# The gate/up product of a SwiGLU feed-forward by one level of Strassen's scheme, with six groups of feed-forward chunks instead of three

## The chip, the cores and the metric

The kernel runs on one core of a Trainium2 chip. The metric is the device time in microseconds of one execution of the whole two-layer trunk. Three runs of the kernel before took 1856.1, 1854.63 and 1850.46 us; the median is 1854.63 us.

The engines are named as the profile names them: PE multiplies matrices, DVE and POOL (GpSimd) and ACT (ScalarE) work elementwise on up to 128 partitions, SP issues the DMAs, and PSUM is the memory into which PE accumulates.

## The reference

One step of a small trunk with 640 tokens (128 context tokens and 512 latent tokens) of width 1024, in fp32. Layer 0 mixes the tokens by differential attention, layer 1 by a gated recurrence; each mixer is followed by a feed-forward of width 2816:

```python
def adanorm(x, g, shift, scale):
    return rmsnorm(x, g) * (1.0 + scale) + shift

def swiglu(h, w_in, w_out):
    gt, up = jnp.split(h @ w_in, 2, axis=-1)
    return (jax.nn.silu(gt) * up) @ w_out
...
        mp = modulation(c_ctx, w_ada[i], b_ada[i])      # six vectors: shift, scale, gate, twice
        ms = modulation(c, w_ada[i], b_ada[i])
...
        xp = xp + mp[2] * op                            # op, os_: the mixer's output
        xs = xs + ms[2] * os_
        xp = xp + mp[5] * swiglu(adanorm(xp, g_norm_ffn[i], mp[3], mp[4]), w_ffn_in[i], w_ffn_out[i])
        xs = xs + ms[5] * swiglu(adanorm(xs, g_norm_ffn[i], ms[3], ms[4]), w_ffn_in[i], w_ffn_out[i])
```

The change concerns `h @ w_in`: a 640x1024 by 1024x5632 product per layer.

## The kernel before

**Numbers.** Every fp32 operand of a large product is split into a high part and a low part in the type fp32r, and a product is three matmuls: high by high, low by high, high by low. For a weight chunk, ACT copies the raw fp32 chunk into the high part (`wh`), and DVE or POOL subtracts that from the raw chunk to get the low part (`wl`); the function is `load_split`. On POOL the subtraction is cut into three instructions. Raw chunks lie in a ring `wr` of 3 buffers of 512 KB, high and low parts in rings `wh` and `wl` of 6 buffers each.

**Feed-forward.** It is `out_and_ffn`, once per layer. The features of h lie on the partitions: `hT` is a pair (`Thi`, `Tlo`) of 8 blocks of 128 features by 640 tokens. The width 2816 is cut into 22 chunks of 128, each called f. For one f, `ffn_chunks` loads two raw chunks of 512 KB (four feature blocks each, the gate and the up columns side by side) and splits both. `ffn_in` then works on one half of the tokens (320) at a time: 24 matmuls into one PSUM sum for the gate, 24 into another for up, both called `psgu`; ACT takes the silu of the gate, DVE multiplies the up sum by it, ACT and DVE split the product into the high and low parts of `gT`. The 22 f's are in three groups:

```python
FF_GROUPS = [(0, 8), (8, 15), (15, 22)]
```

After each group, `rows_out` multiplies `gT` by the rows of `w_ffn_out` of that group: for each half of the 1024 output columns and each of 5 token tiles one PSUM sum `psr` of 128x512, which DVE multiplies by the gate vector (`rtmp`, L1291) and adds to the rows of the residual (L1292).

**Ahead of the first group** the rows of the mixer's output are finished and normalised tile by tile, and each tile is turned by PE (`ntp`), scaled and shifted by DVE and POOL (`ha`, L492 and L493) and split by ACT and DVE (L494, L495) into `hT`; that is `to_hT`. The raw chunks of the first f are asked for when the second token tile is done.

**Work that runs beside the feed-forward.** `fill` is a chain of 64 small steps. The first eight take the last modulation vector of the layer itself: each loads one 512 KB chunk of `w_ada` and multiplies it on PE into the sum `psada`. In layer 0, the others are `summed_units`, modulation vectors of layer 1 computed on DVE: a chunk of `w_ada` is multiplied by the condition and added to an accumulator, which takes two TENSOR_SCALAR (L291) or SCALAR_TENSOR_TENSOR (L293, `acc`) instructions of 128x512 for each feature block, 20 and 140 in all. `take(fill)` issues the next step. It stands after each half of an f and after each tile of `rows_out`, so that the steps are spread over the three groups of layer 0.

**What sets the order.** The kernel is written as one program; a planner then orders the instructions of each engine by its own estimate of durations and due times, and adds the waits. In the places where `pe["strict"]` is set, PE keeps the written order: from the mixer's output until the first f's of the first group. Each engine takes its instructions in the order given; an instruction that waits holds up all that stand behind it on that engine.

## Time and profile before

| what | before |
|---|---|
| median of three runs | 1854.63 us |
| the profiled execution, its span | 1850.6 us (the profile gives no other time of its own for it) |
| PE busy | 1807.3 us, 98% of the span |
| DVE busy | 1081.6 us, 58% |
| ACT busy | 678.6 us, 37% |
| POOL busy | 439.3 us, 24% |
| first gate/up product of layer 0 / of layer 1 | from 437.23 us / from 1390.32 us |
| matmuls of the gate/up product | 4224, all of 128x320 |

Busy time of an engine is the time in which at least one of its instructions ran. Matmuls overlap in the records: one is shown with 309 ns, though another starts every 147 ns; for what a matmul takes of the span, the time of a whole run of them is divided by their number. The granted clock of PE is full from the second of the profile's 40 slices to the last. In layer 0 the feed-forward's groups run from 437 us to 912 us, in layer 1 from 1390 us to the end.

### The profile page before, as it was taken

What the parts mean: (1) busy time and instruction counts of PE and PEld (TensorE: products, weight loads), DVE (VectorE), ACT (ScalarE), POOL (GpSimd) and SP (SyncE); (2) the same over time, 40 slices, a digit from 0 to 9 for tenths busy, and PEclk for the clock granted to TensorE, in tenths of its full rate; (3) what the DMA queues carried; (4) which work ended last, traced back from release to release, by engine and by line L of the source; (5) the groups of instructions that cost most, each with busy time, mean ns of one, the idle gap of its engine ahead of it and who ended that gap; (6) DMA issues with size and microseconds to landing.
All of it is one profiled execution on the core that took longest, in us unless ns stands there. A gap on an engine that the chain in (4) does not pass through costs nothing.

```text
span 1850.6 us, 34604 instructions
## 1 busy us (share of the span) xinstructions
PE 1807.3 (98%) x14064; PEld 1664.6 (90%) x14064; DVE 1081.6 (58%) x1947; ACT 678.6 (37%) x1510; POOL 439.3 (24%) x620
## 2 busy tenths in 40 slices
PE   6999999999999999999999999999999999999998
PEld 5799999778998998999899999998789989998996
DVE  4888888756258546755666666676562333234234
ACT  3567666635231222122533333333352311212221
POOL 3345444325000000000255555555240000000001
PEclk8999999999999999999999999999999999999999
DMA  9511211554364434534422222212242422213211
GB/s 315 174 44 52 72 50 49 167 170 123 96 188 144 130 103 129 168 114 126 140 81 64 64 65 64 64 55 85 84 123 83 149 80 81 69 58 96 87 46 57
DMA packets 218363, 190.02 MB, mean 103 GB/s; under 512 B 9891, under 2 KB 176213, under 8 KB 218204
## 3 DMA queue, kind: packets, MB, share of 16 engines
q1 hardware_dynamic: 217398, 187.22, 32.7%
q8 instruction: 110, 1.80, 0.4%
q10 hardware_dynamic: 806, 0.60, 0.1%
q14 instruction: 49, 0.40, 0.1%
HBM read 180.40 MB, written 7.37 MB: 101 GB/s over the span
## 4 chain that ended last, share of the span: by engine, by line
PE 85%; DVE 7%; DMA 4%; ACT 2%; issue 1%; POOL 1%; SPq 0%; POOLq 0%; ACTq 0%; DVEq 0%
PE psgu L74 31%; PE psr L74 18%; PE psqkv L74 8%; PE psf L74 8%; PE psvg L74 5%; PE pso L74 3%; PE S L74 2%; PE pa L74 2%; PE po L74 1%; DMA wr<-w_ffn_in 1%; PE psada L74 1%; PE ptp L77 1%; DVE Q L1147 1%; DMA wr<-w_ada 1%; DMA ar<-w_ada 1%
## 5 line engine op out<-in xcount | busy, mean ns | idle before, releaser
L74 PE MATMUL psgu<-Tlo,wh 128*128 128x320 f32 x1408 | 435.0, 309 | 1.8 <-DVE Tlo L495 1.8
L74 PE MATMUL psgu<-Thi,wh 128*128 128x320 f32 x1408 | 436.5, 310 | 0.0
L74 PE MATMUL psgu<-Thi,wl 128*128 128x320 f32 x1408 | 434.7, 309 | 0.0
L167 ACT ACTIVATE wh<-wr 128x1024 fp32r<-128x1024 f32 (+1 forms) x224 | 225.9, 1015 | 416.0 <-DMA wr<-w_ffn_in 143.7
L171 DVE TENSOR_TENSOR wl<-wr,wh 128x1024 fp32r<-128x1024 f32 (+2 forms) x146 | 173.5, 1191 | 229.1 <-ACT wh L167 226.3
L74 PEld LDWEIGHTS psgu<-Thi,wh 128*128 128x128 f32 x1408 | 264.2, 188 | 5.7 <-issue 5.3
L74 PEld LDWEIGHTS psgu<-Tlo,wh 128*128 128x128 f32 x1408 | 264.2, 188 | 2.9 <-DVE Tlo L495 2.3
L74 PEld LDWEIGHTS psgu<-Thi,wl 128*128 128x128 f32 x1408 | 264.2, 188 | 0.0
L171 POOL TENSOR_TENSOR wl<-wr,wh 128x341 fp32r<-128x341 f32 (+2 forms) x234 | 218.6, 964 | 183.7 <-ACT wh L167 183.1
L74 PE MATMUL psr<-wh,Thi 128*128 128x512 f32 (+1 forms) x607 | 240.8, 398 | 0.5 <-ACT Thi L503 0.5
L74 PE MATMUL psr<-wh,Tlo 128*128 128x512 f32 (+1 forms) x607 | 235.8, 390 | 0.0
L74 PE MATMUL psr<-wl,Thi 128*128 128x512 f32 (+1 forms) x607 | 234.8, 388 | 0.0
L460 POOL TENSOR_TENSOR nss<-nss 128x1 f32<-128x1 f32 x24 | 7.5, 313 | 855.8 <-ACT xr L455 839.8
L74 PEld LDWEIGHTS psr<-wh,Tlo 128*128 128x128 f32 x607 | 114.3, 188 | 25.1
L74 PEld LDWEIGHTS psr<-wh,Thi 128*128 128x128 f32 x607 | 114.5, 189 | 24.8 <-issue 2.2
L74 PEld LDWEIGHTS psr<-wl,Thi 128*128 128x128 f32 x607 | 114.4, 188 | 21.8
L74 PE MATMUL psf<-Thi,wh 128*128 128x320 f32 x384 | 123.0, 320 | 0.0
L1394 DVE TENSOR_TENSOR gu<-psgu,sil 128x320 f32<-128x320 f32 x88 | 42.8, 486 | 134.0 <-PE psgu L74 134.0
L74 PE MATMUL psf<-Tlo,wh 128*128 128x320 f32 x384 | 118.5, 309 | 0.0
L74 PE MATMUL psf<-Thi,wl 128*128 128x320 f32 x384 | 118.5, 308 | 0.0
L74 PE MATMUL psqkv<-wh,Thi 128*128 128x384 f32 x320 | 109.1, 357 | 1.2 <-ACT Thi L596 1.2
L1291 DVE TENSOR_TENSOR rtmp<-psr,gate 128x512 f32<-128x512 f32 x69 | 47.3, 688 | 102.6 <-PE psr L74 99.4
(250 smaller groups left out, 3440.0 us busy)
## 6 DMA issues: line engine op xcount, KB each, us to landing
wr<-w_ffn_in SPq DMA_DIRECT2D x176, 256.0 KB
wr<-w_ada SPq DMA_DIRECT2D x72, 512.0 KB
wr<-w_ffn_out SPq DMA_DIRECT2D x40, 512.0 KB
wr<-w_in_rec SPq DMA_DIRECT2D x64, 256.0 KB
wr<-w_qkv_attn SPq DMA_DIRECT2D x64, 192.0 KB
ar<-w_ada SPq DMA_DIRECT2D x24, 512.0 KB
gate<-gdram SPq DMA_DIRECT2D x12, 512.0 KB
wr<-w_o_attn SPq DMA_DIRECT2D x8, 512.0 KB
```

Source lines behind the costliest of these rows:

```text
L74: in_order(nc.tensor.matmul(*a, **k))
L77: in_order(nc.tensor.transpose(*a, **k))
L167: nc.scalar.activation(hi[:, :n], r, AF.Copy)
L171: ins = lo_eng.tensor_tensor(lo[:, cs], r[:, cs], hi[:, cs], ALU.subtract)
L460: nc.gpsimd.tensor_tensor(sq[1], sq[0], sq[1], ALU.add)
L1147: nc.vector.tensor_tensor(qview, qview, view(T, n + 1, [2, nb], [-n - 1, 2], [0, m]), ALU.mult)
L1291: nc.vector.tensor_tensor(tmp, ps, gates[0 if t == 0 else 1][:, cs], ALU.mult)
L1394: nc.vector.tensor_tensor(gu, pss[1], sil, ALU.mult)
```

## The change

For one f, the product of the token halves and the feature halves with gate and up is taken as a product of 2x2 blocks: rows are the tokens 0-319 and 320-639, the inner index is the feature halves (blocks 0-3 and 4-7), columns are gate and up. In place of the 8 block products of 4 feature blocks each (12 matmuls each, 96 in all) there are 7 (84 in all), on sums and differences of blocks.

- **The tokens' side, once per layer.** `A1` holds the high and low parts of the tokens 0-319, `A22` those of tokens 320-639 for the feature blocks 4-7, and `S` those of four sums and differences, which lie in the storage of the mixer's output `oT`. `to_rows` takes the place of `to_hT`; `sums` makes the four sums, one addition on POOL and three on DVE per stretch of tokens, in tiles of the tag "row" (3 buffers).
- **The weights' side, for each f.** `ffn_weights` loads the same two raw chunks. POOL makes four differences of 128x512 (L1397 to L1400) into two tiles of the tag "row". Four splits follow (of 512, 1024, 1024 and 1024 elements per partition, ACT L168 and DVE L169), where there were two of 1024.
- **The products.** `ffn_in` is now one routine for both halves of the tokens, with three places for a step of `fill`. Seven products go in the order 1, 2, 6, 5, 7, 3, 4. Three of the sums are carried on in PSUM: `psgu` takes 1, then 6, 7 and 4; `psu` takes 5, then 3; `psg` takes 2. After 1, 6, 5 and 7, ACT copies the sum so far to SBUF (`p1`, `u2`, `p5`, `u3`; L1447 to L1462), and the next product into the same sum follows that copy. DVE adds and multiplies (L1450, L1465, L1466, L1472), POOL adds one (L1463), ACT takes two silus (L1451, L1471), and `out` splits the two results (L1441, L1442) into `gT`.
- **Groups.** Six instead of three: `FF_GROUPS = [(0, 4), (4, 8), (8, 12), (12, 16), (16, 19), (19, 22)]`. `rows_out` thus runs 12 times per layer, not 6; it makes the same number of matmuls for `w_ffn_out`. The second instruction of a row's addition goes to POOL, except in the last half of a layer.
- **`fill`.** A place after each tile of `rows_out` as before, so there are twice as many of these, and three places per f instead of two.
- **The start.** The raw chunks of the first f are asked for after the first three steps of `fill`, not before them. Their low parts are made on DVE, not POOL.
- **Storage.** Gates are loaded in halves of 512 columns; `ha`, `gate`, `rtmp`, `xc` and `acc` share a tag "h" of 7 buffers; `gT` has one buffer, shared with the unsplit `Hf`; the two pools of mixer storage become one; three tables of attention are made in attention's own pool.

The core of the diff:

```diff
-FF_GROUPS = [(0, 8), (8, 15), (15, 22)]
+FF_GROUPS = [(0, 4), (4, 8), (8, 12), (12, 16), (16, 19), (19, 22)]
...
-            def add_rows(ps, t, half, gates):
+            def add_rows(ps, t, half, gates, eng=nc.vector):
...
-                nc.vector.tensor_tensor(xs[t][:, cs], xs[t][:, cs], tmp, ALU.add)
+                eng.tensor_tensor(xs[t][:, cs], xs[t][:, cs], tmp, ALU.add)
...
-                    add_rows(ps, t, half, gates)
+                    add_rows(ps, t, half, gates, nc.gpsimd if after is None else nc.vector)
                     take(fill)
...
+            def sums(c0, c1):
...
+                nc.gpsimd.tensor_tensor(fa[:, 0], a21, a22, ALU.add)
+                nc.vector.tensor_tensor(fa[:, 1], a11, a21, ALU.subtract)
+                nc.vector.tensor_tensor(fb[:, 0], fa[:, 0], a11, ALU.subtract)
+                nc.vector.tensor_tensor(fb[:, 1], a12, fb[:, 0], ALU.subtract)
+                for i, f in enumerate((fa, fb)):
+                    split_rows([v[:, 2 * i : 2 * i + 2, :, c0:c1] for v in S], f)
+
+            def ffn_weights(f):
+                cols = slice(f * P, (f + 1) * P)
+                r1, r2 = (load_raw(wi[:, 4 * c : 4 * c + 4, :, cols], [4, 2, P]) for c in range(2))
...
+                h1 = split(b11, nc.vector, [4, P])
+                h2 = split(x2, nc.vector, [4, 2, P])
+                ta, tb = (xr_tile().rearrange("p (s k c) -> p s k c", s=2, k=4) for _ in range(2))
+                nc.gpsimd.tensor_tensor(ta[:, 0], b12, b11, ALU.subtract)
+                nc.gpsimd.tensor_tensor(ta[:, 1], b22, b12, ALU.subtract)
+                nc.gpsimd.tensor_tensor(tb[:, 0], b22, ta[:, 0], ALU.subtract)
+                nc.gpsimd.tensor_tensor(tb[:, 1], b21, tb[:, 0], ALU.subtract)
+                tb, ta = (
+                    split(t.rearrange("p s k c -> p (s k) c"), nc.vector, [8, P]) for t in (tb, ta)
+                )
...
+            def ffn_in(f, w, group, i):
...
+                sum1 = mm_tile([P, HTOK], "psgu")
+                product(sum1, 1, True)
+                a = part_tile("p1")
+                nc.scalar.activation(a, sum1, AF.Copy)
+                ps = mm_tile([P, HTOK], "psg")
+                product(ps, 2, True)
+                nc.vector.tensor_tensor(a, a, ps, ALU.add)
+                nc.scalar.activation(a, a, AF.Silu)
+                yield
+                product(sum1, 6, False)
...
+                yield
+                product(sum1, 4, False)
...
             for t in range(NT):
...
-                if t == 1:
-                    first = [ffn_chunks(0, nc.gpsimd, l == 0)]
...
                 if gi == 0:
                     take(fill, 3)
-                    first.append(ffn_chunks(1, nc.vector))
-                    to_hT(NT - 2)
-                    ffn_in(0, first[0], gT, 0, 0)
-                    to_hT(NT - 1)
+                    weights = [ffn_weights(0)]
+                    to_rows(NT - 2, nc.vector)
+                    units = [ffn_in(0, weights[0], group, 0)]
+                    take(units[0])
+                    weights.append(ffn_weights(1))
+                    to_rows(NT - 1, nc.vector)
...
                 for f in range(max(f0, 2), f1):
-                    ch = ffn_chunks(f)
-                    for half in range(2):
-                        ffn_in(f, ch, gT, f - f0, half)
+                    for _ in ffn_in(f, ffn_weights(f), group, f - f0):
                         take(fill)
```

Two places show how the order of the instructions moves. The first is SP's order of DMAs at the end of the mixer's output in layer 0. A name such as `wr_5739` is one raw buffer in use; a `w_ffn_in` chunk has two rows because it is loaded by two DMAs of 256 KB. Before:

```order
L69 DMA wr_5571<-w_o_attn 128x2x512 [waits DMAHW2_49,PE_49]
L69 DMA wr_5739<-w_ffn_in 128x4x128 [waits DMAHW7_49,DMAHW3_49,PE_49]
L69 DMA wr_5739<-w_ffn_in 128x4x128
L69 DMA wr_5748<-w_ffn_in 128x4x128 [waits DMAHW5_49,DVE_49]
L69 DMA wr_5748<-w_ffn_in 128x4x128
L69 DMA wr_5943<-w_ada 128x1024 [waits DMAHW6_49,DVE_49]
```

After, with the three chunks of `w_ada` (steps of `fill`) first:

```order
L69 DMA wr_5571<-w_o_attn 128x2x512 [waits DMAHW2_49,PE_49]
L69 DMA wr_5927<-w_ada 128x1024 [waits DMAHW7_49,DMAHW3_49,PE_49]
L69 DMA wr_5933<-w_ada 128x1024 [waits DMAHW5_49,DVE_49]
L69 DMA wr_5939<-w_ada 128x1024 [waits DMAHW6_49,DVE_49]
...
L69 DMA wr_5945<-w_ffn_in 128x4x128 [waits PE_49]
L69 DMA wr_5945<-w_ffn_in 128x4x128
L69 DMA wr_5948<-w_ffn_in 128x4x128 [waits DMAHW5_49,PE_49]
```

The first f's chunks now stand behind the three `w_ada` chunks, and their first DMA waits for PE: for the products `psada` that read the buffer before it. On PE those products stand here in both kernels, after the last `psr` of the mixer's output. What PE has next in the changed kernel, with the single rows of a product left out after its first two:

```order
L74 MATMUL psada_5926<-wr_5939,cT_91 32x256 x4
L77 MATMUL ntp_5973<-ident_66,xr_5845 128x128 x4
...
L74 MATMUL psgu_5999<-A1hi_5609,wh_5951 128x320
L74 MATMUL psgu_5999<-A1lo_5610,wh_5951 128x320
...
L74 MATMUL psada_5926<-wr_6174,cT_91 32x256 x4
L74 MATMUL psgu_6084<-A1hi_5609,wh_6035 128x320
L74 MATMUL psgu_6084<-A1lo_5610,wh_6035 128x320
L74 MATMUL psada_5926<-wr_6197,cT_91 32x256 x4
```

Before, 48 gate/up products in a row follow the first `ntp` pair, and no `psada` stands among them; now further `psada` products, each with a raw chunk of its own, stand between the products of the first two f's.

The second place is DVE in layer 0, amid `fill`. Before, among the f's of the first group:

```order
L1394 TENSOR_TENSOR gu<-psgu,sil 128x320
L291 TENSOR_SCALAR acc<-wr,cT 128x512 x2
L293 SCALAR_TENSOR_TENSOR acc<-wr,cT,acc 128x512
L1396 TENSOR_TENSOR Tlo<-gu,Thi 128x320
L293 SCALAR_TENSOR_TENSOR acc<-wr,cT,acc 128x512 x8
L171 TENSOR_TENSOR wl<-wr,wh 128x1024
```

After, at the end of the first group's `rows_out`s and the start of the second group:

```order
L1317 TENSOR_TENSOR rtmp<-psr,gate 128x512
L169 TENSOR_TENSOR wl<-wr,wh 128x512
L303 SCALAR_TENSOR_TENSOR acc<-wr,cT,acc 128x512 x4
L169 TENSOR_TENSOR wl<-wr,wh 128x1024
L303 SCALAR_TENSOR_TENSOR acc<-wr,cT,acc 128x512 x2
L1450 TENSOR_TENSOR p_7818<-p_7818,psg 128x320
L303 SCALAR_TENSOR_TENSOR acc<-wr,cT,acc 128x512
L169 TENSOR_TENSOR wl<-xr,wh 128x1024
```

There are more splits (`wl`) between the same number of accumulations (`acc`). All 160 `acc` instructions, which before lie in all three groups of layer 0 (22 f's), stand in the changed kernel within the first three of six groups (12 f's).

More of the change, by code (lines that the diff above doesn't have):

```diff
@@ L160, in load_raw, with split @@
         return r[:, :n]
+    def split(src, lo_eng, dims):
+        n = int(np.prod(dims))
+        out = []
+        for name in ("wh", "wl"):
+            v = wp.tile([P, 1024], F32R, name=name, tag=name, bufs=6)[:, :n]
+            if len(dims) == 2:
+                v = v.rearrange("p (a b) -> p a b", a=dims[0])
+            else:
+                v = v.rearrange("p (a b c) -> p a b c", a=dims[0], b=dims[1])
+            out.append(v)
+        nc.scalar.activation(out[0], src, AF.Copy)
+        lo_eng.tensor_tensor(out[1], src, out[0], ALU.subtract)
+        return out
     def load_split(src, dims, lo_eng, ordered=False, slots=None):
@@ L1326, in last_head @@
+            gates = [half_gates(0, half) for half in range(2)]
             def last_head(t):
@@ L1376, in out_and_ffn @@
             nxt = None
[L1378 to L1396 removed]
+            group = {}
```

222 lines of the change are left out of this document (148 added, 74 removed).

## The prediction

> **What bounds the kernel now.** I read the page first (busy shares, the 40 slices, the chain's shares, the product's group), then the chain in order of time, then busy time by stretches of the span.
>
> ```profile
> span 1850.6 us, 34604 instructions
> PE 1807.3 (98%) x14064; PEld 1664.6 (90%) x14064; DVE 1081.6 (58%) x1947; ACT 678.6 (37%) x1510; POOL 439.3 (24%) x620
> DVE  4888888756258546755666666676562333234234
> POOL 3345444325000000000255555555240000000001
> PE 85%; DVE 7%; DMA 4%; ACT 2%; issue 1%; POOL 1%; SPq 0%; POOLq 0%; ACTq 0%; DVEq 0%
> L74 PE MATMUL psgu<-Tlo,wh 128*128 128x320 f32 x1408 | 435.0, 309 | 1.8 <-DVE Tlo L495 1.8
> ```
>
> PE is busy 98% and carries 85% of the chain; so PE bounds, and taking matmuls away shortens the span as long as no other engine fills what is freed. DVE is at 2 to 8 tenths through layer 0's feed-forward (slices 10 to 20) and at 2 to 4 in the last ten, layer 1's; POOL is idle in both places. The last row is one of three such groups of the gate/up product. Its 309 ns is not a matmul's price, since matmuls overlap. The chain has that:
>
> ```profile
> 437.23 7.17 PE psgu L74 x47
> 453.45 20.73 PE psgu L74 x140
> 748.45 3.97 DMA wr<-w_ffn_in
> 1493.56 54.95 PE psr L74 x240
> 1548.51 98.55 PE psgu L74 x672
> ```
>
> 672 products in 98.55 us are 0.1467 us each; an output matmul (`psr`, 128x512) takes 54.95/240 = 0.229 us. One raw chunk of 512 KB, waited for alone, takes about 4 us to come.
>
> ```profile
> core 0: us, PE busy (x) PEld busy (x) DVE busy (x) ACT busy (x) POOL busy (x), PEclk, DMA share, GB/s
> 437.00:912.00 475.00, 474.31 (x3019) 439.44 (x3020) 271.67 (x407) 125.05 (x200) 10.56 (x17) 1.00 0.43 131
> 100.00:330.00 230.00, 229.76 (x1531) 222.06 (x1530) 191.10 (x453) 154.10 (x438) 104.12 (x192) 1.00 0.18 54
> 1549.00:1647.00 98.00, 98.00 (x670) 98.00 (x669) 29.54 (x43) 26.39 (x42) 0.00 (x0) 1.00 0.27 81
> 1038.00:1086.00 48.00, 47.29 (x616) 45.08 (x615) 32.72 (x62) 16.87 (x47) 24.91 (x28) 1.00 0.22 62
> ```
>
> In layer 0's groups (first row) PE loses 0.7 of 475 us, with DVE at 57%; in a group of layer 1 (third) DVE is at 30%. In attention (second) DVE ran at 83% with POOL at 45% and PE still lost nothing. The fourth row is a stretch of layer 1's mixer that I need below.
>
> **The change, part by part.** I add to the median, 1854.63; the profiled span is 4.0 under it.
>
> *Matmuls.* 12 fewer for each of 44 f's: 528 x 0.1467 = **-77.4 us**, if PE stays the bound. At the group's 309 ns it would be 163, which is wrong for the reason above. The output products keep their number.
>
> *The start of each feed-forward.* The rows at which the first f's of layer 0 begin:
>
> ```profile
> 433.05 1.50 PE L74 MATMUL psada<-wr,cT 128*32 128x256 f32 x24
> 433.75 7.74 SPq L69 DMA_DIRECT2D wr<-w_ffn_in  x8
> 437.65 1.06 ACT L167 ACTIVATE wh<-wr 128x1024 fp32r<-128x1024 f32 x1 [0.37 <-DMA wr<-w_ffn_in]
> 440.07 1.06 ACT L167 ACTIVATE wh<-wr 128x1024 fp32r<-128x1024 f32 x1
> 435.27 1.35 POOL L493 TENSOR_TENSOR ha<-ha,adaC 128x512 f32<-128x512 f32 x1 [0.45 <-DVE ha L492]
> ```
>
> Before, these two splits are of the second f; the first f was split long ago. Now the first f's chunks wait until `psada` at 433.05 has read the ring, so they take those places: 437.65 and 440.07. On POOL, behind the second chunk, stand this f's three later differences, the next f's four and a sum, each about 1.35: the first f's end near 444, the last about 452. The next step of `fill` gets its ring slot only near 444 and lands 4 us later; its `psada` stands in PE's order among the second f's products, and three more follow through the ring about 4 us apart: 448, 452, 456, and a last near 460. What is queued on PE behind them are the products of f 0 and 1, and of these only 48 (7 us) stand ahead. By 456 the kernel before had done 47+52+17 = 116 of them, by the chain. So (116 - 48) x 0.147 = 10 us are lost, and about 3 more for the last chunk: **+13 per layer, +26** for both, since layer 1 has the same order. Bounds: +8 each if one chunk more is hidden, +18 if one more is bare. Of the SP queue, the gates and `xc` that now stand behind those three `w_ada` chunks are small and not late by the same row (433.75).
>
> *Layer 0's groups 0 to 2.* These hold all of `fill`'s accumulations. PE needs 12 x 84 x 0.1467 + 360 x 0.229 + some 6 for `psada` = 236 us; with the start, 249. DVE's load, from forms:
>
> ```profile
> L293 DVE SCALAR_TENSOR_TENSOR acc<-wr,cT,acc 128x512 f32<-128x512 f32 x140 | 97.0, 744 | 3.8 <-DMA wr<-w_ada 3.7
> L291 DVE TENSOR_SCALAR acc<-wr,cT 128x512 f32<-128x512 f32 x20 | 8.7, 479 | 0.1
> L171 DVE TENSOR_TENSOR wl<-wr,wh 128x1024 fp32r<-128x1024 f32 x133 | 163.4, 1228 | 227.3 <-ACT wh L167 224.5
> L1291 DVE TENSOR_TENSOR rtmp<-psr,gate 128x512 f32<-128x512 f32 x69 | 47.3, 688 | 102.6 <-PE psr L74 99.4 <-DMA gate<-gdram 3.2
> L1396 DVE TENSOR_TENSOR Tlo<-gu,Thi 128x320 fp32r<-128x320 f32 x88 | 43.8, 497 | 24.7 <-ACT Thi L1395 24.7
> L1135 DVE TENSOR_TENSOR Cn<-Cn,T 128x320 f32<-128x320 f32 x40 | 25.2, 629 | 0.0
> L554 POOL TENSOR_TENSOR orow<-orow,xc 128x512 f32<-128x512 f32 x10 | 13.5, 1353 | 41.4 <-DVE orow L553 41.4
> L167 ACT ACTIVATE wh<-wr 128x1024 fp32r<-128x1024 f32 x184 | 194.9, 1060 | 407.4 <-DMA wr<-w_ffn_in 143.7 <-PE psr L74 120.3 <-PE psf L74 39.0
> L1392 ACT ACTIVATE sil<-psgu 128x320 f32<-128x320 f32 x88 | 38.0, 431 | 129.7 <-PE psgu L74 129.6
> ```
>
> By the order, DVE has there: 140 `acc` (97.0), 20 (8.7), 30 `rtmp` (20.6), 50 low parts of 1024 (61.4) and 13 of 512 (9), 72 of 320 wide (35), and some 20 at the start: 242 us. To this comes POOL. It was idle here (10.56 of 475) and now makes 76 instructions of 512 at 1.353 and 12 of 320 at 320/512 of that (0.85) or a little more, 114 us. How the two disturb each other shows in
>
> ```profile
> 435.64 1.53 DVE L495 TENSOR_TENSOR Tlo<-ha,Thi 128x512 fp32r<-128x512 f32 x1
> 437.88 0.68 DVE L495 TENSOR_TENSOR Tlo<-ha,Thi 128x512 fp32r<-128x512 f32 x1
> 438.09 3.35 POOL L493 TENSOR_TENSOR ha<-ha,adaC 128x512 f32<-128x512 f32 x2
> 1360.53 2.04 POOL L493 TENSOR_TENSOR ha<-ha,adaC 128x512 f32<-128x512 f32 x2 [2.15 <-DVE ha L492]
> ```
>
> The same DVE subtraction takes 1.53 beside POOL's of 435.27, and 0.68 where POOL's next began later; POOL's two take 3.35 beside DVE, 2.04 without. Instructions with two operands in SBUF lengthen each other. For the size I take L1135, 629 ns in the stretch of the fourth window row, where POOL is busy 24.91 of 48 us (0.52), against 497 for L1396 at the same width: 0.13 us each. I count 259 DVE instructions of that kind, so 34 us; scaled to POOL's share here (114 of 249, 0.46 for 0.52), 30; and as POOL's instructions are 512 wide where L1135's neighbours were shorter, I raise it by half to 45, less 10 that successive DVE instructions overlap: 277 us. Bounds of this term: none (242) and twice (about 330). So DVE passes PE's 249. An engine fed by DMA, ACT and PSUM isn't filled to the last: 83% in the second window row, where it still bounded nothing. Between 83% and 100% I take 92%: 277/0.92 = 301, **+52** over 249. Bounds: +3 (no disturbance, 96% filled) to +85 (83% filled). PE then waits for low parts (`wl`) behind `acc` on DVE, and raw chunks come late because `acc` holds their ring.
>
> The Trainium skill, "SBUF — State Buffer", section "Who interferes with whom", has a rule for this: a DVE instruction with two SBUF inputs and a GpSimd instruction that reads SBUF exclude each other. The 1.53 and 0.68 agree.
>
> *Later groups.* With no `acc` left, DVE has per f about 4.2 of low parts and 3 of others, 7 us, against 12.3 of PE; ACT 3.7 of splits, four copies and silus of 0.43 and more, 8 us. **0**, hidden under PE.
>
> *Sums carried on in PSUM.* Product 6 may not start before ACT has copied `psgu`; one other product (12 x 0.147 = 1.76 us) stands between. A split on ACT ahead of the copy takes 1.06, the copy 0.43, and the matmul's end lags its issue by 0.16: 1.65, just hidden. Two splits in a row cost 0.9. Such meetings in one f of five: 44/5 x 0.9 = **+8**; bounds 0 and 35 (nearly every f).
>
> *The rest at nothing:* row additions on POOL (nobody on PE waits for them; their price lies in the port term), gates by halves (a DMA of the same bytes, asked for a group ahead), twelve `rows_out` (same matmuls), pools and tables (no instruction more in a loop). If POOL lags, the next group's `h` buffers are late, but 7 are there.
>
> Sum: -77.4 + 26 + 52 + 8 = **+8.6**, so **1863 us**.
>
> **The rivals.**
>
> *B, faster: DVE's work fits in the gaps.* If POOL and DVE disturb each other little and DVE stays under PE, the fourth term is +3: -77.4 + 26 + 3 + 8 = -40, **1814 us**. The point from which it decides: a DVE need, idle included, of 249 us in groups 0 to 2. For it: attention's 83% with PE lossless. Against: DVE would have to be 97% filled even undisturbed.
>
> *C, the shared operand path is held for whole instructions.* Then DVE's two-operand work (97 + 61.4 + 9 + 23.5 = 191) and POOL's 114 exclude each other: 305 us of that path alone, at 92% 332, +83 in place of 52: **1894 us**. For it: 1.53 against 0.68, as long as a whole POOL instruction. Against: L1135's mean lengthening is a quarter. This is what the rule of the Trainium skill, "SBUF — State Buffer", "Who interferes with whom", gives if taken literally: an exclusive lock.
>
> *D, even the start is hidden.* -77.4 + 8: **1785 us**. Against: `psada` in PE's order and one ring of three.
>
> *E, ACT's copies stall PE in every f.* 44 x 1 = 44 in place of 8: **1899 us**. Against: ACT is at 27% in the third window row.
>
> **How the numbers follow.** Forecast 0.52, B 0.26, C 0.10, D 0.06, E 0.06. About 0.3% (5.6 us) is what a measurement can tell from no change. The forecast's own range is 1839 to 1886 (fill 98% and start 20; fill 87% and start 32); of its 0.52, 0.08 lies below 1849, 0.12 within, 0.32 above. Faster: 0.08 + 0.26 + 0.06 = 0.40; same 0.12; slower 0.32 + 0.16 = 0.48. Cases of both signs are held, so the range goes from B's lower part to beyond C: 1808 to 1902, leaving out D and the ends of B and E.
>
> **What would show it.** In the changed profile: products at 0.147 us in undisturbed runs of the chain (else the first term falls); layer 0's first long product run beginning about 13 us later; in layer 0's groups 0 to 2 a DVE busy over 85% and a stretch of about 300 us, PE's idle ahead of `psgu` named as DVE `wl`; in groups 3 to 5 and all of layer 1 a PE with no idle. The forecast is wrong on the fast side if that stretch is near 250 us, and on the slow side if PE also waits in layer 1's groups for ACT or POOL.

## The result, and the profile after

The changed kernel takes 1954.36 us (median of four runs, 1950.08 to 1958.23) against 1855.32 us before (median of four): a ratio of 1.0545, 95% interval 1.0523 to 1.0566. It is 99 us slower. The forecast was 1863 us, with a range up to 1902 us: the sign that it held likeliest, but the size far off, and outside the range. The profiled execution took 1953.84 us, its span is 1952.1 us.

The page of the changed kernel, the rows that answer to those of before:

```profile
span 1952.1 us, 34748 instructions
PE 1787.6 (92%) x13524; PEld 1615.1 (83%) x13524; DVE 1351.2 (69%) x2167; ACT 815.9 (42%) x1778; POOL 941.5 (48%) x936
DVE  4888888657679688765675666666758656555665
PEclk8999999997978888899999999999998999999998
PE 71%; DVE 12%; DMA 7%; POOL 4%; issue 3%; ACT 2%; SPq 0%; POOLq 0%; DVEq 0%; ACTq 0%
```

PE's share of the chain falls from 85% to 71%; DVE's, the DMAs' and POOL's rise. The granted clock is below full in the tenth slice and from the twelfth to the seventeenth, in layer 0's feed-forward, and once more where layer 1's begins. To place the loss I cut the trace into stages by their first products:

| stage | before, us | after, us | difference |
|---|---|---|---|
| start to the first gate/up product of layer 0 | 435.7 | 438.6 | +2.9 |
| layer 0's feed-forward, to the first `psf` of layer 1's mixer | 486.7 | 589.0 | +102.3 |
| layer 1's mixer | 452.0 | 454.8 | +2.8 |
| layer 1's feed-forward, to the end | 476.2 | 469.7 | -6.5 |

Each feed-forward has 264 products fewer, 38.7 us. So layer 0 lost 141 us to something else and layer 1 lost 32 us. Busy time in two stretches, groups 0 to 2 of layer 0 and layer 1 behind its start:

```profile
core 0: us, PE busy (x) PEld busy (x) DVE busy (x) ACT busy (x) POOL busy (x), PEclk, DMA share, GB/s
512.00:800.00 288.00, 224.86 (x1244) 189.72 (x1243) 230.53 (x285) 73.76 (x130) 108.98 (x69) 0.86 0.40 126
1550.00:1940.00 390.00, 385.94 (x2265) 357.63 (x2263) 231.56 (x283) 154.68 (x265) 222.67 (x156) 1.00 0.30 92
```

In the second, PE is busy 99% at full clock with POOL at 57%: where no `fill` runs, the product scheme costs PE next to nothing. In the first, no engine is full (DVE 80%, POOL 38%) and PE idles 22% of the time at a clock of 0.86.

What PE lost can be counted from the starts of its matmuls. A start that comes over 0.3 us later than usual I call a gap; smaller excess is slow issue. Layer 0's feed-forward before: 2.4 us of gaps and 12.6 of slow issue; after: 112.7 and 44.0. The difference, 141.7, agrees with the loss above. The slow issue is 31.4 of it, more than a fifth: matmuls that ran slow behind gaps, as in the first of these pieces of the chain:

```profile
459.51 2.96 PE psgu L74 x10
478.53 3.42 PE psgu L74 x22
530.72 1.76 PE psgu L74 x12
```

10 products in 2.96 us are 0.30 us each, behind a wait for `psada`; 22 in 3.42 are 0.155, and 12 in 1.76 are 0.147, where PE had been busy for some time.

The longest of what PE, ACT, SP and DVE waited for between 437 and 850 us (total, times, longest wait in us):

```profile
PE psr L74 <- ACT wh L177: 31.8, 4, 13.8
PE psgu L74 <- ACT wh L168: 12.0, 8, 3.0
PE psada L74 <- DMA wr<-w_ada: 10.4, 3, 5.9
PE psg L74 <- DVE wl L169: 9.1, 7, 2.6
PE psgu L74 <- DVE wl L169: 7.9, 5, 2.9
PE psgu L74 <- ACT u L1455: 4.1, 3, 1.6
...
ACT wh L177 <- DMA wr<-w_ffn_out: 62.2, 10, 16.5
ACT wh L168 <- DMA wr<-w_ffn_in: 57.2, 18, 8.3
...
SPq L69 <- DVE acc L303: 111.2, 29, 16.4
SPq L69 <- DVE wl L169: 64.6, 21, 10.3
...
DVE wl L169 <- ACT wh L168: 27.0, 12, 8.7
```

Read together, these waits make a circle. PE waits for the high and low parts of weights, longest before `psr`, for the high parts of `w_ffn_out`; ACT, which makes the high parts, waits for raw chunks to come; SP doesn't ask for them, because the ring's buffer is still to be read by DVE (`acc`, `wl`); and DVE stands in its own order behind low parts whose high parts ACT hasn't made. One turn of it in the chain:

```profile
547.09 3.52 DMA wr<-w_ffn_out
550.64 1.06 ACT wh L177
...
568.65 3.42 DMA wr<-w_ffn_in
572.20 1.27 POOL xr L1397
573.48 1.67 POOL orow L1318
...
577.92 1.56 POOL xr L1398
579.48 2.24 POOL xr L1399
581.79 1.28 POOL xr L1400
583.10 1.06 ACT wh L168
```

From the start of one f's first load to the last split of its weights pass 15 us and more, on three engines, with a row addition between POOL's differences; PE needs 12.3 us for an f, and the ring's three buffers hold one f and a half.

The durations of the same stretch (437 to 850 us, by shape):

```profile
L303 DVE SCALAR_TENSOR_TENSOR acc<-wr,cT,acc 128x512 f32<-128x512 f32 x140 | 122.3, 911 | 8.0 <-DMA wr<-w_ada 8.0
L169 DVE TENSOR_TENSOR wl<-xr,wh 128x1024 fp32r<-128x1024 f32 x32 | 43.9, 1376 | 9.3 <-ACT wh L168 9.3
L169 DVE TENSOR_TENSOR wl<-wr,wh 128x1024 fp32r<-128x1024 f32 x16 | 28.6, 1787 | 5.6 <-ACT wh L168 5.6
L1399 POOL TENSOR_TENSOR xr<-wr,xr 128x512 f32<-128x512 f32 x16 | 28.3, 1768 | 4.3 <-DVE Tlo L1355 3.1 <-DVE wl L169 1.2
L1317 DVE TENSOR_TENSOR rtmp<-psr,gate 128x512 f32<-128x512 f32 x30 | 20.1, 682 | 16.9 <-PE psr L74 11.3 <-issue 5.6
L301 DVE TENSOR_SCALAR acc<-wr,cT 128x512 f32<-128x512 f32 x20 | 17.1, 886 | 0.5 <-DMA wr<-w_ada 0.5
```

On average `acc` rose from 744 to 911 ns, low parts of 1024 from 1228 to 1376 and 1787, POOL's 512 wide from 1353 to 1768 (L1399). `rtmp`, with one operand in PSUM, stayed at 682 (688 before). A mean hides two kinds here; the accumulators' rows of the same stretch, with the shortest, median and longest duration in ns:

```profile
L303 DVE SCALAR_TENSOR_TENSOR acc<-wr,cT,acc x140: 734/740/1787, 487.5 to 795.4; 128x512 f32<-128x512 f32 x140
L301 DVE TENSOR_SCALAR acc<-wr,cT x20: 471/487/1524, 486.2 to 780.3; 128x512 f32<-128x512 f32 x20
```

Of the 140, 110 took 734 to 780 ns, as before the change; all but one of them started while POOL ran nothing. The other 30 took 1.54 us on average. Each of these started while a POOL instruction ran and ended 0.55 us after that one's end: it had been held until then. In all that is 24 us.

### The profile page after: what moved, and what is told of

Its sections match the earlier page's. It is cut to its first block, busy times and chain, and to the rows that moved or that the text cites. A ratio compares the mean times of both kernels' runs of the same rounds, so it can differ in the third digit from the quotient of the medians.

```text
span 1952.1 us, 34748 instructions
## 1 busy us (share of the span) xinstructions
PE 1787.6 (92%) x13524; PEld 1615.1 (83%) x13524; DVE 1351.2 (69%) x2167; ACT 815.9 (42%) x1778; POOL 941.5 (48%) x936
## 4 chain that ended last, share of the span: by engine, by line
PE 71%; DVE 12%; DMA 7%; POOL 4%; issue 3%; ACT 2%; SPq 0%; POOLq 0%; DVEq 0%; ACTq 0%
PE psr L74 17%; PE psgu L74 12%; PE psqkv L74 8%; PE psf L74 8%; PE psu L74 7%; PE psvg L74 5%; DMA wr<-w_ada 3%; DVE acc L303 3%; PE psg L74 3%; PE pso L74 2%; PE S L74 2%; DVE wl L169 2%; PE pa L74 2%; DMA wr<-w_ffn_in 1%; PE po L74 1%
## 5 line engine op out<-in xcount | busy, mean ns | idle before, releaser
L74 PE MATMUL psr<-wh,gT 128*128 128x512 f32 (+1 forms) x886 | 289.3, 399 | 34.6 <-ACT wh L177 31.8
L74 PEld LDWEIGHTS psr<-wh,gT 128*128 128x128 f32 x886 | 168.1, 191 | 75.5 <-ACT wh L177 33.3
L177 ACT ACTIVATE wh<-wr 128x1024 fp32r<-128x1024 f32 (+2 forms) x136 | 133.0, 985 | 203.6 <-PE psgu L74 76.6
L1318 POOL TENSOR_TENSOR orow<-orow,rtmp 128x512 f32<-128x512 f32 x110 | 174.0, 1608 | 81.0 <-DVE rtmp L1317 81.0
L74 PE MATMUL psr<-wl,gT 128*128 128x512 f32 (+1 forms) x443 | 174.4, 394 | 1.8 <-DVE wl L181 1.8
L1463 POOL TENSOR_TENSOR u<-u,p 128x320 f32<-128x320 f32 x44 | 59.9, 1362 | 238.2 <-ACT u L1462 229.2
L169 DVE TENSOR_TENSOR wl<-xr,wh 128x1024 fp32r<-128x1024 f32 x88 | 133.7, 1522 | 49.0 <-ACT wh L168 49.0
L169 DVE TENSOR_TENSOR wl<-wr,wh 128x512 fp32r<-128x512 f32 x88 | 120.6, 1373 | 57.1 <-ACT wh L168 56.9
L168 ACT ACTIVATE wh<-wr 128x512 fp32r<-128x512 f32 x88 | 74.2, 845 | 180.0 <-PE psr L74 59.8
L303 DVE SCALAR_TENSOR_TENSOR acc<-wr,cT,acc 128x512 f32<-128x512 f32 x140 | 122.3, 911 | 8.0 <-DMA wr<-w_ada 8.0
L168 ACT ACTIVATE wh<-xr 128x1024 fp32r<-128x1024 f32 x88 | 92.0, 1057 | 85.4 <-PE psr L74 32.7
L1397 POOL TENSOR_TENSOR xr<-wr 128x512 f32<-128x512 f32 x44 | 69.1, 1571 | 115.1 <-DMA wr<-w_ffn_in 97.2
L74 PE MATMUL psgu<-Thi,wh 128*128 128x320 f32 x352 | 111.6, 318 | 7.1 <-ACT u L1455 4.1
L74 PE MATMUL psu<-Tlo,wh 128*128 128x320 f32 x352 | 111.9, 318 | 0.0
```

Source lines behind the costliest of these rows:

```text
L74: in_order(nc.tensor.matmul(*a, **k))
L168: nc.scalar.activation(out[0], src, AF.Copy)
L169: lo_eng.tensor_tensor(out[1], src, out[0], ALU.subtract)
L177: nc.scalar.activation(hi[:, :n], r, AF.Copy)
L303: nc.vector.scalar_tensor_tensor(acc[g], w, c, acc[g], ALU.mult, ALU.add)
L1318: eng.tensor_tensor(xs[t][:, cs], xs[t][:, cs], tmp, ALU.add)
```

## The experiments

All times are medians; each run's "before" was timed beside it on the same chip, 1853 to 1855 us. The stage times are those of the table above: F0 is layer 0's feed-forward (589.0 in the changed kernel, 486.7 before), F1 layer 1's (469.7 and 476.2). Edits are against the changed kernel unless another is named.

**One remedy at a time.** The first four kernels each undo or take away one part.

Spread fill:

```diff
+    def spaced(gen, dense):
+        for n, _ in enumerate(gen):
+            yield
+            if n >= dense:
+                yield
...
+            fill = spaced(fill, 13)
```

> After the first 13 steps, every second place for a step of fill is left empty, so that the 160 accumulations of layer 0 lie in about 19 f's instead of 12; nothing else is changed. Crowding (too much DVE work per f of groups 0 to 2, whatever POOL does): of the about 109 us lost there behind the start, at least 70 come back, time 1860 to 1885. Operand sharing (each DVE instruction is lengthened by POOL's new work, which is the same per f): what DVE needs in all is the same, the loss moves to later groups, time 1925 to 1950. Late ring (raw chunks of w_ada keep the 3 buffers): also relieved, 1870 to 1900, but then the idle time ahead of PE is named as a DMA of w_ffn_in or w_ffn_out, not as a DVE low part.

Measured: 1986.52 us, ratio to before 1.0718 (1.0702 to 1.0734): 32 us slower than the changed kernel, F0 623.4. All three expectations miss. DVE's load went down (between 512 and 800 us it was busy 208 of 288 us, not 231) and PE idled 50 us there, not 63; but the steps now disturb the later f's as well: between 850 and 1000 us PE was busy 122 of 150 us, where it had been 148.

Without the first three steps of fill:

```diff
-                    take(fill, 3)
                     weights = [ffn_weights(0)]
```

> The three steps of fill ahead of the first f are left out, so that the raw chunks of the first f are asked for first, as in the kernel before, in both layers. Start order theory: the starts lost about 34 us in layer 0 and 31 in layer 1 (gaps and slow matmuls); they fall by 12 to 25 each, time 1905 to 1930. If instead POOL's chain of differences and the sums set the start, each falls by less than 6: 1942 or more. Layer 1 tells it apart, since its fill is only these steps.

Measured: 1936.27 us, 1.0452 (1.0436 to 1.0468). F0 572.7, 16 less; F1 470.9, 1 more. The time lies between the two expectations. In layer 1, which was to tell it apart, the order of the first loads isn't what sets the start. In layer 0 most of the 16 lie behind the start: PE idled 17 us between 437 and 512 us, where it had been 22, and 50 between 512 and 800, where it had been 63.

Without POOL's four differences:

```diff
-                nc.gpsimd.tensor_tensor(ta[:, 0], b12, b11, ALU.subtract)
... three more
-                tb, ta = (
-                    split(t.rearrange("p s k c -> p (s k) c"), nc.vector, [8, P]) for t in (tb, ta)
-                )
+                tb, ta = (split(r.rearrange("p (a c) -> p a c", c=P), nc.vector, [8, P]) for r in (r2, r1))
```

> Leaves out POOL's four differences for each f; the splits of 1024 read the raw chunks instead, so the sums are of other numbers. ACT, DVE and PE have the same instructions, POOL loses about 69 of 88 instructions of 512 and 320 wide per group-of-12 stretch less the row additions. Operand sharing theory: DVE's acc falls from 911 ns to about 780 and the low parts to 1250, groups 0 to 2 win 50 or more, time 1870 to 1900. Crowding theory: DVE's own work stays, 1920 to 1940. In layer 1, whose groups lose nothing, neither expects a change but at the start.

Measured: 1920.98 us, 1.0363 (1.0345 to 1.0382). F0 568.6, F1 459.1: 20 and 11 us less. `acc` fell to 855 ns, the splits of 512 from 1243 to 793, those of 1024 to 1260 (between 500 and 850 us). The time is at the edge of the crowding expectation. So sharing is real, but taking most of it away, and with it the weights' line through POOL, brings 33 us back, of the 177 that are lost (99 slower, and 77 not saved).

Row additions on DVE:

```diff
-                    add_rows(ps, t, half, gates, nc.gpsimd if after is None else nc.vector)
+                    add_rows(ps, t, half, gates, nc.vector)
```

> The second instruction of a row's addition goes back to DVE everywhere. Operand sharing theory: 30 POOL instructions of 1.6 us fewer in groups 0 to 2 against 30 of 0.65 us more on DVE: 5 to 25 us faster, 1930 to 1950. Crowding theory: 20 us more DVE work where DVE bounds, 10 to 30 slower, 1964 to 1985.

Measured: 1955.26 us, 1.0547 (1.0529 to 1.0564); F0 589.1. Neither: with the additions on it DVE was busy 228 us between 512 and 800, with POOL's share of them 231; what it gained from POOL's absence it spent on the work.

**Loads, accumulations, groups.**

No loads of `w_ada` for layer 1's vectors:

```diff
-                r = load_raw(wa[:, k : k + 2, c0 : c0 + 512], [2, 512])
                 for i in range(2):
-                    w = r[:, 512 * i : 512 * i + 512]
+                    w = ident.unsqueeze(1).to_broadcast([P, 4, P])
```

> The 40 raw chunks of w_ada for layer 1's vectors are not loaded: the 160 accumulations read the identity matrix, stretched to 512 columns, so the vectors are of other numbers. DVE's work is the same, in number and width; the ring of 3 raw buffers is then left to the feed-forward's own chunks. Ring theory (each chunk of w_ada takes a buffer that the next f's chunks then wait for, 4 us of load at a time, and behind a late chunk stands the whole line of split, four differences, split): of the about 105 us lost between 512 and 800 us at least 75 come back, time 1860 to 1885. DVE theory (accumulations crowd DVE or are lengthened by POOL): nearly nothing comes back, 1930 or more.

Measured: 1951.59 us, 1.0528 (1.0511 to 1.0546); F0 583.4. By the expectation the ring theory falls. But PE's wait changed its name; here is its longest between 512 and 860 us, and busy time in one piece of it:

```profile
PE psada L74 <- DVE acc L303: 76.5, 6, 19.8
...
560.00:620.00 60.00, 47.66 (x298) 43.64 (x297) 56.21 (x72) 17.35 (x29) 19.75 (x13) 0.87 0.17 55
```

With the loads gone DVE is busy 94% in this piece (81% from 512 to 800 us), and PE stands before `psada`, whose accumulators DVE hasn't finished. One bound was taken away and another stood right behind it.

Fewer accumulations:

```diff
-                    for g in range(2):
+                    for g in range(2 if k + i == 0 else 1 - i):
```

> Of 160 accumulations 50 are kept; all 40 chunks of w_ada are loaded as before, and the vectors are of other numbers. Ring theory: a chunk's buffer is freed 2 us sooner (load 4, wait, four accumulations of 0.9), about a third of its time there: 25 to 50 us come back, 1905 to 1930. DVE theory: 110 x 0.9 = 99 us of DVE's work go, nearly all that was lost comes back, 1860 to 1880.

Measured: 1937.3 us, 1.045 (1.0434 to 1.0466); F0 575.5. The DVE theory falls too, as the only one: 99 us of its work gone bring 17. The ring theory's 25 us aren't reached either.

Own buffers for the chunks of `w_ada`:

```diff
-                r = load_raw(wa[:, k : k + 2, c0 : c0 + 512], [2, 512])
                 for i in range(2):
-                    w = r[:, 512 * i : 512 * i + 512]
+                    w = raw_tile()        # fp.tile([P, 512], F32, tag="fr", bufs=2)
+                    load(out=w, in_=wa[:, k + i, c0 : c0 + 512])
```

> The chunks of w_ada for layer 1's vectors are loaded into two buffers of their own, of 256 KB each, one feature block at a time; the ring of 3 is the feed-forward's alone. For the space, the tag h has 5 buffers, not 7. Ring theory: 60 to 90 us faster than the changed kernel, 1865 to 1895. DVE theory: same as the changed kernel, 1940 or more. If the 5 buffers of h cost something, layer 1 shows it, which has no such chunks.

Measured: 1956.74 us, 1.0548 (1.0532 to 1.0565); F0 585.7. As in the run without loads, the wait only changed its name. ACT's waits for `w_ffn_out` and `w_ffn_in` between 437 and 850 us, 62.2 and 57.2 us in the changed kernel, are 2.4 and 5.9 here, and PE's longest is

```profile
PE psada L74 <- DVE acc L303: 59.8, 6, 19.8
```

Layer 1's feed-forward took 469.0, so the 5 buffers of `h` cost nothing there. For layer 0, whose accumulators lie in `h` too, that doesn't settle it. SP's waits ahead of the gate loads, which need a buffer of `h`, were 17 us in this stretch, 28 in the changed kernel; no run has 5 buffers alone.

Six groups in the kernel before:

```diff
-FF_GROUPS = [(0, 8), (8, 15), (15, 22)]
+FF_GROUPS = [(0, 4), (4, 8), (8, 12), (12, 16), (16, 19), (19, 22)]
...
-                    if f == 6:
+                    if f == 3:
+                        take(fill, 2)
                         gates = load_gates(gate_tile, l, 1)
```

> The kernel before with the six groups, and no Strassen; two steps of fill are moved ahead of the first group's output so that its gates are ready. Both theories: chunks of w_ada stand closer together (about 53 steps in three of six groups), but an f's chunks are done after one split each, without POOL's line: within 1% of before, 1850 to 1872. If it loses 30 us or more, the grouping, and not the product's scheme, carries the loss.

Measured: 1900.6 us, 1.0253 (1.0237 to 1.0268), 48 slower than before: F0 521.7 (+35.0), F1 487.7 (+11.5). Outside the range of both expectations, and past the 30 us from which it was to speak against the grouping. The groups alone, without the product scheme and without any new work on POOL, cost nearly half as much as the changed kernel's 99 us; that they are half of those 99 isn't shown by it.

**Two remedies together.** Since each edit of the changed kernel alone moved the time by -33 to +32 us and the wait only changed its name, the next theory was that several things set about the same time, so that only taking away all of them shows.

Own buffers and spread fill (both edits above):

> Both remedies together: the chunks of w_ada in two buffers of their own, as in the run with the own ring, and the steps of fill spread, as in the run with the spread fill. Two-bounds theory: in groups 0 to 2 two things each set about the same time, DVE's crowded work and the ring of 3 with its loads, so that either remedy alone shows nothing; together they win 70 to 110 us over the changed kernel, 1845 to 1885. Queue theory (any step of fill, wherever it stands, holds PE, ACT or DVE up by its place in an order that was planned with shorter durations, about 2.5 us a step): no win, 1940 to 1990.

Measured: 1930.29 us, 1.0415 (1.0397 to 1.0433); F0 555.6. Of the changed kernel's 589.0 the one alone had taken 3 and the other added 34; together they take 33. They need each other, as the theory says, but the time falls by 24 us, a third of what it expected at least. It lies between the ranges of the two theories.

The same without the first three steps of fill:

> As the run before in this list, and without the three steps of fill ahead of the first f. Two-bounds theory: 15 to 20 us less than that run, as they were without it, 1828 to 1868, and this may pass the kernel before. Queue theory: 1920 to 1970.

Measured: 1936.65 us, 1.0449 (1.0432 to 1.0466); F0 561.8. The two-bounds theory misses, and the time is inside the queue theory's range: the 16 us that this edit had brought alone are gone.

A quarter of fill:

```diff
             for k in range(0, KT, 2):
+                if k > 0:
+                    yield
+                    continue
                 r = load_raw(wa[:, k : k + 2, c0 : c0 + 512], [2, 512])
```

> Of the 40 chunks of w_ada for layer 1's vectors 10 are loaded and 40 of 160 accumulations made, in the same places; the other steps are empty, and the vectors are of other numbers. Two-bounds theory: DVE and ring are both relieved: 70 to 100 us faster than the changed kernel, 1855 to 1885. Queue theory at 2.5 us a step: 30 steps fewer, 75 us, the same; the run only says how much the fill carries in all, against the start of each layer and the product itself. If it stays over 1910, the loss is not the fill's.

Measured: 1880.14 us, 1.0146 (1.013 to 1.0161); F0 517.1. Three quarters of layer 1's vectors carry 72 us of layer 0's 141. Both theories had this time in their ranges.

Own buffers and fewer accumulations:

> The chunks of w_ada in two buffers of their own, and 50 of 160 accumulations (the vectors are of other numbers); places of the steps unchanged. Two-bounds theory: both bounds are relieved, 60 to 100 us faster than the changed kernel, 1855 to 1895. Queue theory: as each alone, 1930 or more.

Measured: 1916.05 us, 1.0343 (1.0325 to 1.0362); F0 542.2: 47 less, where the two alone took 3 and 14. Again more than their sum, again less than the two-bounds theory expected.

**Where the rest is.** Own buffers, spread fill and no differences on POOL:

> Own buffers for the chunks of w_ada, fill spread, and POOL's four differences left out (the splits read the raw chunks; sums of other numbers). Three-bounds theory: the weights' line through POOL is the third bound of layer 0, hidden behind the two others so far: 35 to 60 us less than with own buffers and spread fill (1930), 1870 to 1895, of which about 10 is layer 1's start. If POOL's part is only the lengthening of DVE: 20 to 33 less, as without the remedies, 1897 to 1910.

Measured: 1884.78 us, 1.0166 (1.015 to 1.0183); F0 524.5, F1 461.7. 45.5 us below the run with the two remedies: within the three-bounds expectation. Its busy time where the changed kernel had PE at 78%:

```profile
512.00:800.00 288.00, 270.19 (x1639) 242.91 (x1638) 211.34 (x285) 104.77 (x180) 68.44 (x47) 0.99 0.43 129
```

PE is at 94%, the clock at 0.99, and DVE at 73%. The fill is spread, so 98 of the 160 accumulations stand in this stretch, where the changed kernel has 147. Layer 0 isn't free of loss with all three away: without any, F0 would be 448 (486.7 less 38.7), and it is 77 us more.

The scheme in layer 1 only (layer 0's feed-forward is the function of the kernel before, with three groups, called from the changed kernel's file):

```diff
+FF_GROUPS_0 = [(0, 8), (8, 15), (15, 22)]
...
-    hT, xr = out_and_ffn(0, oT, w_o, open_rows, gsub, o_tiles, reg, x_in)
+            hT, xr = out_and_ffn_rows(0, oT, w_o, open_rows, gsub, o_tiles, regA, regB, x_in)
```

> Layer 0's feed-forward as in the kernel before (rows scheme, three groups); layer 1's as in the changed kernel (7 products, six groups). Layer 1 has no accumulations and no chunks of w_ada behind its start. If the product itself loses nothing on PE and the start costs about 32 us there: 38.7 saved, 32 lost, 1854 - 7 = 1847, and the span between the end of layer 1's start and the end of the program holds no idle PE. If layer 1's gain in the changed kernel came from something in layer 0 (a late start that hides other work), 1854 or more.

Measured: 1845.88 us, ratio 0.9956 (0.994 to 0.9972): 8.6 us faster than before, where 7 were expected. The 7 were the changed kernel's own layer 1 carried over (38.7 saved, 32 lost), so the agreement says that layer 1's gain doesn't hang on layer 0. Between 1450 and 1840 us, behind layer 1's start, PE is busy 386.28 of 390 us.

The same, with the first two f's differences on DVE:

```diff
+                de = nc.vector if f < 2 else nc.gpsimd
-                nc.gpsimd.tensor_tensor(ta[:, 0], b12, b11, ALU.subtract)
+                de.tensor_tensor(ta[:, 0], b12, b11, ALU.subtract)
... the same for the other three
```

> As the run before in this list, and for the first two f's of layer 1 DVE makes the four differences, not POOL. Line theory of the start (POOL's differences at 1.6 us each, one behind the other, and the DVE instructions that they lengthen, hold the first S and weight parts back): 5 to 12 us less than that run, 1836 to 1843. DVE theory of the start (DVE is filled with the sums and low parts there): 8 more DVE instructions, 0 to 6 us more.

Measured: 1844.6 us, 0.9946 (0.9933 to 0.996). No different from the run before, so the line theory falls: in the start the differences cost as much on DVE as on POOL. Left out altogether, they bring layer 1 11 us, by the run without them. This is the fastest kernel of the study, and together with the run before the only one that beats both the kernel before and the changed one: 9.9 us faster than before, about 110 faster than the changed kernel.

The same, without the first three steps of fill in layer 1:

```diff
-                    take(fill, 3)
                     weights = [ffn_weights(0)]
```

> As the run with the scheme in layer 1 only and the first two f's differences on DVE, and without the three steps of fill ahead of the first f in layer 1. Shared-path theory of the start (DVE's and POOL's instructions with two operands in SBUF exclude each other, so it is their sum that sets the start, wherever they run): no change from the order of the loads, within 4 of 1845. Load-order theory: 8 to 15 us less, 1830 to 1837.

Measured: 1854.16 us, 0.9997 (0.9988 to 1.0006): 10 us slower than with these steps, and neither theory expected that. In the profiled executions 6 of the 10 lie in layer 1's feed-forward (474.6 against 468.2) and 4 ahead of layer 0's first product (438.4 against 434.7), which stands ahead of the edit. Pieces of its chain at layer 1's start:

```profile
1381.28 3.30 PE psgu L75 x11
...
1389.50 1.35 DVE xr L1401
...
1404.88 2.10 DVE wl L170
...
1407.67 1.07 ACT Thi L1355
...
1412.86 3.30 PE psu L75 x15
```

The products of the first f begin early, at 1381, but the first one that needs a sum of tokens begins at 1409; from 1387.8 to 1407.6 everything on the chain is DVE, instruction after instruction: sums, differences, low parts. With the steps of fill first, the chain of the changed kernel goes through the loads and POOL to the same point:

```profile
1490.27 1.57 POOL xr L1399
...
1493.20 3.82 DMA wr<-w_ada
...
1497.06 1.12 PE psada L74 x8
...
1498.20 3.66 DMA wr<-w_ada
...
1510.43 4.99 DMA wr<-w_ada
...
1516.55 5.44 PE psu L74 x22
```

Six groups in the kernel before, with spread fill (`fill = spaced(fill, 24)`):

> The kernel before with six groups (1901), and behind the first 24 steps every second place for a step of fill left empty: the accumulations reach from f 4 to f 21 and are no longer crowded into f's 4 to 14. Crowding theory of that run's loss: 20 to 35 us come back, 1866 to 1880, the rest being layer 1's 11. If the grouping itself costs (a raw chunk of w_ffn_out and a change between products and rows twice as often, in layer 0 beside fill): within 8 of 1901.

Measured: 1888.7 us, 1.0182 (1.0169 to 1.0195), 12 below the run with six groups; F0 509.3. Between the two expectations: crowding is a third of the 35 us that layer 0 lost there; the rest is not.

## Why the prediction was wrong

The terms of the sum, as forecast and as the changed kernel's trace has them. What was lost is counted from the starts of the matmuls as above, less the same count of the kernel before; "behind the start" begins at 512 us:

| term | forecast, us | measured, us |
|---|---|---|
| matmuls | -77.4 | -77.4 (not measured alone; 0.147 each holds) |
| starts of the two feed-forwards | +26 | +29 and +28 |
| layer 0's groups 0 to 2 behind the start | +52 | +101 |
| copies of running sums | +8 | at most 4, within the row above |
| end of layer 0's feed-forward, from 850 us | 0 | +12 |
| end of the program, behind the last matmul | 0 | +6 |
| sum | +8.6 | +99 |

**The matmuls: right.** -77.4 us by 0.1467 us each. The products run at 0.147 in undisturbed parts, as the chain shows (12 in 1.76 us), and behind layer 1's start PE is busy 99%.

**The start: the mechanism half right, the size too small.** Forecast +13 per layer, bounds 8 to 18; measured 34 us of gaps and slow issue up to 512 us in layer 0 (4.6 before) and 31 in the first 62 us of layer 1's feed-forward (4 before). The line of `w_ada` chunks through the ring stood as forecast and came later still: 448, 452, 456 and 460 us were given, and the chain of the changed kernel has

```profile
453.61 1.12 PE psada L74 x8
458.43 1.08 PE psada L74 x8
...
471.26 1.08 PE psada L74 x8
```

What the step left out is that the sums of the tokens' side (`sums` and their splits) hold the first product that needs them as long as that line does: the run in layer 1 without the first steps shows DVE's work from 1381 to 1409 us in the line's place. It also took slow matmuls behind a gap at their full speed: 9.2 us of layer 1's start are slow issue.

**Layer 0's groups 0 to 2: the step that failed.** +52 was forecast, bounds 3 to 85; PE lost 77.5 us of gaps and 31.4 of slow issue between 512 and 850 us, 109 in all, against 8 before. The groups took 372 us (438.6 to 810.7), where 301 were forecast. The working was a sum of durations on one engine, divided by a filling of 92%. The durations were not the fault: DVE was busy 291 us in these groups, forecast 277, though POOL was busy 156, forecast 114. The fault was to take DVE as the only bound and to let one number, 92%, stand for everything else: the filling was 78%. Nor was PE's wait the one that was named. It waited 18.8 us before `psgu`, `psg` and `psu` for `wl`, and longest, 31.8 us, before `psr` for the high parts of `w_ffn_out`, whose raw chunks had not come.

The runs show no single bound there: the ring of raw chunks, DVE's accumulations, and POOL's line of differences, each one away alone, bring 3, 14 and 20 us of F0; own buffers with spread fill bring 33, own buffers with fewer accumulations 47, and own buffers, spread fill and no differences 64. PE's wait passes from one to the other, as the run without loads and the one with own buffers showed. That ring, ACT and DVE wait for each other in fixed orders is read from the waits; no run took the orders themselves away. So taking these three away together brings back 64 of the 141 us that layer 0 lost; where the other 77 go stays open, beyond the start and the end named here.

**And slow matmuls.** Of the 109 us, 31.4 are slow issue behind gaps. The prediction's price for a wait was its length.

**The groups.** The prediction put twelve `rows_out` at nothing. Six groups in the kernel before cost 48 us: 35 in layer 0, of which 12 are the crowding of fill by the run with spread fill, and 11.5 in layer 1. About half of the 11.5 is the end of the program, in the changed kernel too. The last matmul before and after, of spans of 1850.6 and 1952.1 us:

```profile
1841.63 0.28 PE L74 MATMUL psr<-wh,Tlo 128*128 128x256 f32 x1
1937.12 0.28 PE L74 MATMUL psr<-wh,gT 128*128 128x256 f32 x1
```

So 8.9 us of other work stood behind it before, 14.9 now, and 14.6 in both runs of the kernel before with six groups. In a last group of 3 f's PE needs 9 x 0.229 = 2.1 us for a tile of rows, in one of 7 it needed 4.8, and on the chain before the finishing of a tile takes 4.7 us (the `rtmp` of successive tiles stand at 1827.84 and 1832.55). PE thus runs ahead of the finishing, which is left over at the end; that cause is read from these rows, no run changed the last group alone. Of the 23 us in layer 0 that spread fill doesn't bring back, PE loses 7 up to 512 us, 9 between and 7 in the last 70 us; why wasn't found, and the kernel before needed its gates earlier for the test, which may be part of them. How much of it the changed kernel pays is open, since its order is another: in its layer 1, between the start and the end, PE loses next to nothing with the same six groups.

The gates by halves were put at the same bytes. By the page they are 56 loads of 256 KB, where 12 of 512 KB stood before. Between 437 and 850 us SP stood 26.3 us before them for POOL's row additions, once for 21.4, with raw chunks behind them in its order. With the additions on DVE it stood 38.9 us there and F0 was the same; no run took these loads away.

**Copies of running sums: the mechanism right, hidden more than forecast.** Forecast +8; PE waited 4.1 us for `u` between 437 and 850 us, and none of its waits in layer 1 is for a copy.

**The later groups: right but for their end.** Between 850 and 1000 us PE is busy 147.85 of 150 us, in layer 1 behind its start 99%. From 1000 to 1028 us, where layer 0's last rows are finished, it is 21.78 of 28.

**The rivals.** B (DVE's work fits in the gaps) fell: 372 us, not 249. C (the operand path is held for whole instructions) came nearest in time, with 1894, and its mechanism is there: the 30 long `acc` were held until a POOL instruction ended. The forecast's 0.13 us for each instruction was the mean of held and free ones. But it isn't what bounds the groups: POOL or a DVE instruction without an operand in PSUM ran in 301 of the 372 us, and with POOL's differences gone the time was still 1921. E (copies stall in every f) fell. None of them was several bounds at the same height. The sign was forecast right, slower at 0.48 against faster at 0.40; it came from a term whose working failed, so it says little for the forecast.

## What to carry to other kernels

When a stage has slack on its helpers and a change uses up several of them at once, adding up the busiest engine isn't enough: list every shared thing that the stage's items pass (ring slots, queues, engines), give each its time per item, and where two or three come near the bound, expect more loss than any one of them gives, and little from relieving one. When two engines hold each other up, look at single instructions before taking a mean: held and free ones are two kinds. Price a wait of the matrix engine at more than its length, as the matmuls behind it run slow. Look at the end of the program as well, where shorter groups leave work behind the last matmul. And try a change first in the part of the program where nothing runs beside it: here the same scheme wins 9 us in layer 1 alone and loses 99 in both layers.

## What the runs showed of the hardware

Matmuls behind gaps were slow: 0.267 to 0.30 us apart where the usual is 0.147 (0.267: ten products from 703.58 to 705.98 us), and the granted clock of the stretch 512 to 800 us was 0.86. A wait of 2.19 us was enough: after full clock from 726 us on, PE waited from 736.3 to 738.5 us for a `wl`, and the clock was 1.00 from 735 to 739 us, 0.50 from 739.5 to 749.5 and 1.00 again from 749.5 to 756. The Trainium skill, "TensorE: Matmul & The Clock Gate", section "HAM oscillation — how this bites in real kernels", has such a loss: an array that waits again and again between bursts of matmuls is set back to half its clock and each burst starts slow. It ties this to waits of more than about 3.4 us. This trace agrees in kind, 44 us in layer 0's feed-forward, but not in that length, by the 2.19 us above; what the shortest such wait is, no run here was made to show.

A DVE instruction with its operands in SBUF that started while POOL ran was held until POOL's instruction ended, not slowed in part: 30 of the 140 two-operand `acc` took 1.54 us on average and ended 0.55 us after POOL's, the others 734 to 780 ns. The one-operand TENSOR_SCALAR of 512 did the same: 479 ns before, and now 9 of the 20 took up to 1524 ns and ended 0.28 us after a POOL instruction, the others 471 to 496. The Trainium skill, "SBUF — State Buffer", section "Who interferes with whom", names `tensor_scalar` among the operations that can take the pair of ports shared with GpSimd; the row agrees. With an operand in PSUM (`rtmp`, 682 ns) nothing changed.
